# A hybrid layer on one core: the MLP seam in two column parts, norm rows further down TensorE's order, weights split ahead

## The chip, the cores and the metric

The kernel runs on one core of a Trainium2 chip. The metric is the device time of one execution in microseconds, lower is better. The times of several runs are given with their median.

## The reference

One layer of a streaming encoder in fp32, for x of 1024 tokens by 1024 channels and 256 memory tokens. There are three sub-layers, each with an RMS norm before and after it, added to the residual:

```python
# 1. token mixers on one normalised input h
q, k, v, u, gate_attn, gate_ssm = split(h @ w_in)
A = stick_breaking_attention(q, k, v)      # 8 heads x 64, strictly causal
B = s5_branch(u, ...)                      # 32 groups of 16 channels, 64 complex states each,
                                           # linear recurrence over time, GELU, y * sigmoid(y @ w_glu + b_glu)
x1 = x + norm((sigmoid(gate_attn) * (A @ w_ba) + sigmoid(gate_ssm) * (B @ w_bs)) @ w_out)
# 2. cross-attention of 4 heads x 256 into 256 memory tokens
x2 = x1 + norm(memory_cross_attention(norm(x1), mem_n, wq, wk, wv, wo))
# 3. gated MLP, d_ff = 2816, with a causal depthwise convolution of width 3 between
up = conv(norm(x2) @ w_up) + conv_b
out = x2 + norm((gelu(gate) * val) @ w_down)
```

## The kernel before

Every fp32 product is made of three TensorE passes on rounded parts (`mm3`, L139 to L142): high by high, high by low and low by high. So each weight chunk is loaded (`ws`), cast to its high part on ScalarE (ACT) (`wh`) and subtracted to its low part on VectorE (DVE) (`wl`), and each intermediate that enters a product is split the same way (`split`, L144). The names in the profile are those of the tiles: `ps_f`, `ps_z`, `ps_p` and so on are PSUM banks by tag, `hT` is the normalised input turned to channels by tokens.

Up to the end of the second sub-layer's query projection the order of TensorE, ACT, DVE and POOL is written by hand as a list of events with a planned time. `pe(took, go)` puts a TensorE step at the planner's clock and advances it; `at(t, go)` puts any other step at the time t; `plan(t, took, go, n)` puts a turn or the like into TensorE's order once the clock has come to t; `all_events` then issues all of it in order of time. The times are a plan and not a schedule: each engine runs its own instructions in the order issued, and waits where an operand isn't there.

The stages, in order: norm and turn of x with the projections to v and u; the SSM stage; the stick-breaking attention (units of a head and query blocks: scores, `weigh`); the memory's keys and values (`mem_k`, `mem_v`); the branch products with their gates; `mix_out` with w_out, in two halves of 512 tokens; the rows x1; `xa_query`; the cross attention; the output units 0 to 3 with w_o; the MLP.

In the SSM stage a slot (SLOT = 12.2 on the planner's clock) holds one of eight groups: `states` (L666, the input terms), a chain of DVE instructions with the scan (L675 to L687), `outputs` (L700, L701, which read the readout matrices F and the scanned `rc`). `operators` makes W (L602 to L604), `readout` makes F (L612 to L614), `intra` makes the part inside a chunk (L620), all on DVE first. Matmuls of the gates' projection (`gate_job`, chunks `weights`) fill TensorE between them:

```python
        def weights(self, t0, hi=5.0, lo=3.8):
            for dt_, go in ((14.0, self.load), (hi, self.high), (lo, self.low)):
                at(t0 - dt_, go)
```

The rows x1 of a half begin when its last `mix_out` step is done (`rows_x1`): x1_load, sum, square, norm rate, norm (`xr`, L1348), and then `turn_x1`, which turns the row on TensorE (L1355) and splits it (L1358, L1359). Matmuls of the next half, or of `xa_query`, stand between the turns.

In the cross attention `xa_score` and `xa_weigh` go two units apart, and `Fill` gives out filler matmuls (the query projection, or w_o of output unit 0) between their steps: `Fill(steps, 32, 16)` is two filler steps for each gap.

The MLP's up-projection is a Strassen-Winograd product of 2 x 2 blocks: seven products per pair of weight chunks (gate and value), with left operands A11, A12, S4, A22, S1, S2, S3 from the turned rows (`quad`) and right operands `bm` (L1752 for pair 0). The seam is pair 0: its products 1, 2, 5, 6, 3, 7 run in column parts, since the last output unit (unit 3) yields its tokens only now. `product(p, prod, cols)` (L1805) makes one of them: 12 matmuls (L1815, L1817, L1818) and its eviction from PSUM into `uu` (L1827 to L1834). The chain that the last part needs is: rows of unit 3 (`rows`), its two turns (`turn`, L1632) and the operands of its columns. After the seam, TensorE goes on with products of pair 1 and after it, and the convolution of pair 0 (`c_scale`, `c_tap`, `c_gelu`, L1921, L1925) runs in slots between them on ACT and DVE.

## Time and profile before

| what | value |
| --- | --- |
| three runs, median (lowest, highest) | 1708.67 us (1708.15, 1709.71) |
| profiled execution: time, span | 1710.89 us, 1709.1 us |
| mean granted TensorE clock | 0.995 of full speed |
| TensorE (PE) busy | 1658.4 us, 97% |
| VectorE (DVE) busy | 1137.8 us, 67% |
| ScalarE (ACT) busy | 865.4 us, 51% |
| GpSimd (POOL) busy | 225.3 us, 13% |

The span is from the first to the last instruction. Busy is the time in which an engine runs an instruction; TensorE's matmuls overlap, so their durations are longer than their spacing. A wait is idle time ahead of an instruction, put down to what came last. PEclk in the windows is the clock that TensorE was granted, as a share of full speed.

The stages lie at about these times: x and v, u up to 85 us; SSM from 85 to 260; attention to 568; memory to 614; branches and w_out to 802; cross attention from 831 to 976; units 1 to 3 to 1049.8; seam to 1082.3; the rest of the MLP to the end.

### The profile page before, as it was taken

The page shows a single profiled execution, that of the slowest core. Times are in us where ns is not written, and L with a number is a line of the kernel's source. Part 1 is how long each engine was busy: PE and PEld are TensorE (multiplying, and loading weights), DVE is VectorE, ACT ScalarE, POOL GpSimd, SP SyncE. Part 2 cuts the span into 40 slices and gives each one's busy share as a digit, 9 for nine tenths or more (in the row PEclk, how much of TensorE's full clock was granted, in tenths as well). Part 3 has the DMA queues.
Part 4 walks back from the last instruction along what each step waited for, and adds up shares of the span by engine and source line. Part 5 has one row for each costly group of instructions (what it writes and reads, how often), then busy time and mean ns, then how long its engine had stood idle before and what let it go on. Part 6 is the DMA issues. An engine that isn't in the chain of part 4 may idle for free.

```text
span 1709.1 us, 22655 instructions
## 1 busy us (share of the span) xinstructions
PE 1658.4 (97%) x8244; PEld 1393.4 (82%) x8244; DVE 1137.8 (67%) x1565; ACT 865.4 (51%) x1459; POOL 225.3 (13%) x247
## 2 busy tenths in 40 slices
PE   7999999999999999999999998999999999999998
PEld 6897887888888878887788887878888888788886
DVE  7718855866776655446645677788888887965473
ACT  5414444666666543235534455555555555653441
POOL 5000001433332000000221001011111111000010
PEclk9999999999999999999999999999999999999999
DMA  7002134332333774444512576386777776787572
GB/s 290 26 26 68 50 107 124 80 100 71 97 109 107 266 241 133 166 160 160 185 62 99 178 253 224 88 245 185 199 214 209 219 200 187 220 287 262 195 230 91
DMA packets 119792, 274.14 MB, mean 160 GB/s; under 512 B 21761, under 2 KB 26241, under 8 KB 119553
## 3 DMA queue, kind: packets, MB, share of 16 engines
q1 hardware_dynamic: 110320, 254.61, 44.7%
q0 software_dynamic: 9360, 18.09, 6.0%
q8 instruction: 65, 1.06, 0.3%
q14 instruction: 47, 0.38, 0.1%
HBM read 196.76 MB, written 67.37 MB: 155 GB/s over the span
## 4 chain that ended last, share of the span: by engine, by line
PE 46%; DVE 4%; DMA 2%; ACT 1%; issue 1%; POOL 0%; SPq 0%; DVEq 0%; POOLq 0%; ACTq 0%
PE ps_p L1815 7%; PE ps_p L1818 7%; PE ps_p L1817 7%; PE ps_d L2075 4%; PE ps_d L2074 4%; PE ps_d L2076 4%; PE ps_m L140 2%; PE ps_m L142 1%; PE ps_m L141 1%; PE ps_p L141 1%; PE ps_p L142 1%; PE ps_p L140 1%; PE ps_a L141 1%; PE ps_a L142 1%; PE ps_a L140 1%
## 5 line engine op out<-in xcount | busy, mean ns | idle before, releaser
L140 PE MATMUL ps_f<-hT,wh 128*128 128x512 f32 x384 | 166.8, 434 | 1.3 <-ACT wh L273 1.3
L142 PE MATMUL ps_f<-hT,wl 128*128 128x512 f32 x384 | 152.4, 397 | 3.6 <-DVE wl L277 3.6
L141 PE MATMUL ps_f<-hT,wh 128*128 128x512 f32 x384 | 151.7, 395 | 0.0
L1815 PE MATMUL ps_p<-qS,bm 128*128 128x512 f32 (+2 forms) x380 | 143.9, 379 | 3.9 <-DVE uu L1834 3.9
L1817 PE MATMUL ps_p<-qS,bm 128*128 128x512 f32 (+2 forms) x380 | 143.8, 378 | 0.0
L1818 PE MATMUL ps_p<-qS,bm 128*128 128x512 f32 (+2 forms) x380 | 143.7, 378 | 0.0
L146 DVE TENSOR_TENSOR dn<-raw,dn 128x1024 fp32r<-128x1024 f32 x77 | 93.8, 1223 | 66.5 <-ACT dn L145 64.2
L933 DVE TENSOR_TENSOR_SCAN s<-s,zcol 128x128 f32<-128x128 f32 (+3 forms) x96 | 106.4, 1109 | 37.9 <-ACT s L928 37.1
L145 ACT CAST dn<-raw 128x1024 fp32r<-128x1024 f32 x77 | 80.9, 1054 | 92.2 <-PE ps_d L2076 36.9
L939 POOL TENSOR_TENSOR s<-s,s 128x127 f32<-128x127 f32 (+4 forms) x96 | 92.2, 962 | 252.1 <-DVE s L933 208.8
L2074 PE MATMUL ps_d<-dn 128*128 128x512 f32 x308 | 119.8, 389 | 0.0
L2075 PE MATMUL ps_d<-dn 128*128 128x512 f32 x308 | 119.8, 389 | 0.0
L2076 PE MATMUL ps_d<-dn 128*128 128x512 f32 x308 | 119.8, 389 | 0.0
L1815 PE MATMUL ps_p<-qA,bm 128*128 128x512 f32 (+2 forms) x280 | 106.5, 380 | 1.7 <-DVE uu L1834 1.3
L1818 PE MATMUL ps_p<-qA,bm 128*128 128x512 f32 (+2 forms) x280 | 106.4, 380 | 0.7 <-DVE bm L1752 0.7
L1817 PE MATMUL ps_p<-qA,bm 128*128 128x512 f32 (+2 forms) x280 | 106.3, 379 | 0.0
L1764 POOL DMA_DIRECT2D bm<-in_ffn_up_T x61 | 53.4, 876 | 354.5 <-ACT bm L1763 185.6
L1829 ACT COPY uu<-ps_p 128x512 f32<-128x512 f32 (+2 forms) x93 | 52.0, 559 | 84.2 <-PE ps_p L1818 84.1
L142 PEld LDWEIGHTS ps_f<-hT,wl 128*128 128x128 f32 x384 | 72.7, 189 | 20.8 <-DVE wl L277 4.4
L1815 PEld LDWEIGHTS ps_p<-qS,bm 128*128 128x128 f32 x380 | 72.2, 190 | 17.9 <-DVE uu L1834 3.1
L209 POOL TENSOR_TENSOR rstd<-rstd,mhalf 128x1 f32<-128x1 f32 x42 | 29.2, 700 | 436.8 <-DMA raw<-td 174.0
L1818 PEld LDWEIGHTS ps_p<-qS,bm 128*128 128x128 f32 x380 | 72.1, 190 | 13.1
(520 smaller groups left out, 4469.3 us busy)
## 6 DMA issues: line engine op xcount, KB each, us to landing
raw<-sd SPq DMA_DIRECT2D x77, 256.0 KB, 3.3
bm<-in_ffn_up_T POOLq DMA_DIRECT2D x61, 256.0 KB, 5.6
ws<-in_w_in_T SPq DMA_DIRECT2D x24, 512.0 KB, 3.4
ws<-in_xa_wo_N SPq DMA_DIRECT2D x23, 512.0 KB, 4.2
wv<-in_ffn_up_T SPq DMA_DIRECT2D x22, 512.0 KB, 4.3
wg<-in_ffn_up_T SPq DMA_DIRECT2D x22, 512.0 KB, 4.1
dr<-in_ffn_down SPq DMA_DIRECT2D x22, 512.0 KB, 6.7
td<-st SPq DMA_DIRECT2D x44, 256.0 KB, 6.3
```

The costliest lines, as they stand in the source:

```text
L140: T.matmul(acc, sh, mh, start=first, stop=False)
L141: T.matmul(acc, sh, ml, start=False, stop=False)
L142: T.matmul(acc, sl, mh, start=False, stop=last)
L146: (lo or V).tensor_tensor(dl, src, f(dh), op=ALU.subtract)
L933: V.tensor_tensor_scan(s2[:, n0:n1][:, ::-1], s2[:, n0:n1][:, ::-1], zcol.to_broadcast([P, n1 - n0]), 1.0 if diag else s2[:, n1:n1 + 1], o ...
L939: G.tensor_tensor(s1[:, n0:e], s1[:, n0:e], s2[:, n0 + 1:e + 1], op=ALU.mult)
L1815: T.matmul(acc, bm[:, 0, ks], q[:, 0, k, cols], start=alone and k == 0, stop=False, skip_group_check=True)
L1817: T.matmul(acc, bm[:, 0, ks], q[:, 1, k, cols], start=False, stop=False, skip_group_check=True)
L1818: T.matmul(acc, bm[:, 1, ks], q[:, 0, k, cols], start=False, stop=k == 3, skip_group_check=True)
L2074: T.matmul(acc[i], v[:, 0, 0, sl], v[:, 0, 1], start=first, stop=False, skip_group_check=True)
L2075: T.matmul(acc[i], v[:, 0, 0, sl], v[:, 1, 1], start=False, stop=False, skip_group_check=True)
L2076: T.matmul(acc[i], v[:, 1, 0, sl], v[:, 0, 1], start=False, stop=last, skip_group_check=True)
```

## The change

- At the start, the second weight chunk's high and low part come after the first parts of `hT`.
- SSM stage: gate weights are loaded, cast and subtracted 5.2 earlier on the planner's clock. `operators(1)` and `readout(2)`, `readout(3)` come before the first slot, and each later one is a step further ahead; W has two buffers and F four. `intra` is planned at 1.75 instead of 0.5.
- The last `weigh` of the attention is held back and put behind twelve matmuls of `mem_k`. The first half of the branch weights is split 4 earlier, and the second half's loads are issued 4.1 earlier.
- x1: the chain of a row starts 5.5 instead of 8.0 ahead, its turn is planned at 8.5 instead of 6.5, the second half's pace is 5.0 instead of 4.0, and five chunks of `xa_query` instead of four run beside it.
- Cross attention: TensorE's order is by hand from its start, as it was from unit 1 of the output. The first and last group of four units give out about 1.5 filler steps per gap, so that the last group's filler also reaches the last two weighs. `rows` makes both rows of a unit in one generator, with one power on POOL.
- Seam: the column parts are (0 to 384, 384 to 512) instead of (0 to 256, 256 to 384, 384 to 512). Product 3 of the first part is made in two pieces (S4a and S4). The low operands of products 5 and 6 come after unit 3's last evictions.
- After the seam, the convolution steps of pair 0 come two slots later.

```diff
@@ -277,7 +277,7 @@
         def weights(self, t0, hi=5.0, lo=3.8):
-            for dt_, go in ((14.0, self.load), (hi, self.high), (lo, self.low)):
+            for dt_, go in ((9.0 + hi, self.load), (hi, self.high), (lo, self.low)):
@@ -439,7 +439,7 @@
             at(s0 + 2.4, lambda _, t=t: x_load(t + 4))
-    for c, (t0, t1) in enumerate(((6.3, 8.3), (7.8, 8.9), (10.4, 11.9), (12.0, 13.2))):
+    for c, (t0, t1) in enumerate(((6.3, 8.3), (9.5, 10.7), (10.4, 11.9), (12.0, 13.2))):
@@ -594,7 +594,7 @@
         pool = open_t.pool
-        wof[o] = W = pool.tile([P, 8, 8, 16], F32, tag="W", name="W")
+        wof[o] = W = pool.tile([P, 8, 8, 16], F32, tag="W", name="W", bufs=2)
@@ -607,7 +607,7 @@
         gs = slice(4 * n, 4 * n + 4)
-        fof[n] = F1 = pool.tile(sh4, F32, tag="F1", name="F1", bufs=2)
+        fof[n] = F1 = pool.tile(sh4, F32, tag="F1", name="F1", bufs=4)
@@ -749,6 +749,9 @@
     at(82.0, lambda t: readout(t, 1))
+    at(88.0, lambda t: operators(t, 1))
+    at(94.0, lambda t: readout(t, 2))
+    at(98.0, lambda t: readout(t, 3))
@@ -775,7 +778,7 @@
             if ns in first_of:
-                first_of[ns].weights(clock, *((3.8, 2.7) if ns == 64 else (5.0, 3.8)))
+                first_of[ns].weights(clock, *((3.8, 2.7) if ns == 64 else (10.2, 9.0)))
@@ -785,7 +788,7 @@
-    plan(70.0, 0.5, intra, 0)
+    plan(70.0, 1.75, intra, 0)
@@ -803,16 +806,17 @@
                 plan(s0 + SLOT, 0.9, states, n + 1)
-                if n:
-                    at(s0 + 6.4, lambda t, n=n: readout(t, n + 1))
+                if 1 <= n <= 4:
+                    at(s0 + 6.4, lambda t, n=n: readout(t, n + 3))
...
                 at(s0 + 8.5, lambda t, o=o: tables(t, o + 2))
+            if not q and o < 2:
+                at(s0 + 8.5, lambda t, o=o: operators(t, o + 2))
             if not q and o < 3:
-                at(s0 + 8.5, lambda t, o=o: operators(t, o + 1))
-                plan(s0 + SLOT, 0.5, intra, o + 1)
+                plan(s0 + SLOT, 1.75, intra, o + 1)
@@ -1042,6 +1046,7 @@
+    held = groups.pop()
@@ -1157,7 +1162,7 @@
-    at(clock + 1.2, lambda _: open_c())
+    at(clock + 3.2, lambda _: open_c())
@@ -1166,9 +1171,9 @@
         at(clock + 8.0 + 2.8 * i, lambda _, i=i: branch_load(0, i))
-        at(clock + 18.0 + 2.8 * i, lambda _, i=i: branch_high(0, i))
-        at(clock + 19.2 + 2.8 * i, lambda _, i=i: branch_low(0, i))
-        at(clock + 20.6 + 2.8 * i, lambda _, i=i: branch_load(1, i))
+        at(clock + 14.0 + 2.8 * i, lambda _, i=i: branch_high(0, i))
+        at(clock + 15.2 + 2.8 * i, lambda _, i=i: branch_low(0, i))
+        at(clock + 16.5 + 2.8 * i, lambda _, i=i: branch_load(1, i))
@@ -1215,6 +1220,8 @@
             pe(0.36, mem_k, ch, m, k)
+            if (m, k) == (0, 3):
+                pe(held[3], held[1], *held[2])
@@ -1358,12 +1365,12 @@
-    PACE = 5.4, 4.0
+    PACE = 5.4, 5.0
     def rows_x1(t, r0_):
-        line(r0_ - 8.0, (lambda: x1_load(t), 8.0), (lambda: x1_sum(t), 1.4),
+        line(r0_ - 5.5, (lambda: x1_load(t), 5.5), (lambda: x1_sum(t), 1.4),
...
-        plan(r0_ + 6.5, 0.9, turn_x1, t)
+        plan(r0_ + 8.5, 0.9, turn_x1, t)
...
@@ -1410,9 +1417,9 @@
                            for k2 in range(2) for i in range(4)]
-    for m in range(4):
+    for m in range(5):
         ch = Chunk(a["xa_wq_T"][m])
-        steady += [(ch if k == 0 else None, xa_query, (ch, m, k), False) for k in range(KT)]
+        steady += [(ch if k == 0 else None, xa_query, (ch, m // 4, m % 4, k), False) for k in range(KT)]
...
@@ -1518,27 +1528,35 @@
         ysl = yu[u][i][:, dh * 512:(dh + 1) * 512]
-        C.activation(ysl, acc[i], AF.Square, accum_out=su[u][i][:, dh:dh + 1])
+        C.activation(ysl, acc[i], AF.Square, accum_out=su[u][:, dh, i:i + 1])
...
-    def rows(u, i):
-        y, t = yu[u][i], 2 * u + i
-        xr = p6.tile([P, D], F32, tag="xn", name="xr", bufs=2)
-        dma(xr, x1_d[t])
+    def rows(u):
+        xr = [p6.tile([P, D], F32, tag="xn", name="xr", bufs=2) for _ in range(2)]
+        for i in range(2):
+            dma(xr[i], x1_d[2 * u + i])
         yield
...
+        r, o = (p6.tile([P, 2], F32, tag="r2" + n, name="r2" + n, bufs=2) for n in "ab")
+        V.tensor_tensor(r, su[u][:, 0], su[u][:, 1], op=ALU.add)
+        V.tensor_scalar(r, r, 1.0 / D, EPS, op0=ALU.mult, op1=ALU.add)
+        G.tensor_tensor(o, r, mhalf.to_broadcast([P, 2]), op=ALU.pow)
         yield
-        ss = p6.tile([P, 2], F32, tag="ss", name="ss", bufs=3)
-        C.activation(xr, y, AF.Square, accum_out=ss[:, 0:1])
...
@@ -1584,6 +1602,8 @@
+    by_hand = ctx.enter_context(ExitStack())
+    by_hand.enter_context(tc.manual_schedule(engines={mybir.EngineType.PE}))
@@ -1591,7 +1611,7 @@
-            fill = Fill(steps, 32, 16)
+            fill = Fill(steps, 32 if n else 24, 16 if n < 12 else 22)
@@ -1679,14 +1699,8 @@
     operand(hb, "hb", "A12")
-    by_hand = ctx.enter_context(ExitStack())
-    by_hand.enter_context(tc.manual_schedule(engines={mybir.EngineType.PE}))
     def both(u):
-        gs = [rows(u, 0), rows(u, 1)]
-        for _ in range(4):
-            for g in gs:
-                pump(g)
+        drain(rows(u))
@@ -1800,29 +1814,32 @@
     FULL = slice(0, 512)
+    PART = slice(0, 384), slice(384, 512)
...
-        bm, q = ops[p, prod], quad["S4a" if prod == 3 and cols.stop == 256 else LEFT[prod]]
+        bm = ops[p, prod]
+        pieces = [(quad[LEFT[prod]], cols, cols)]
+        if prod == 3 and cols == PART[0]:
+            pieces = [(quad["S4a"], slice(0, 256), slice(0, 256)), (quad["S4"], slice(256, 384), slice(256, 384))]
...
         whole = accs[p, {1: 1, 6: 1, 7: 1, 4: 1, 2: 2, 5: 5, 3: 5}[prod]]
-        acc = whole[:, cols]
         alone = prod in (1, 2, 5) or (p, prod) == (0, 4)
-        for k in range(4):
-            ks = slice(k * P, (k + 1) * P)
-            T.matmul(acc, bm[:, 0, ks], q[:, 0, k, cols], start=alone and k == 0, stop=False,
-                     skip_group_check=True)
-            T.matmul(acc, bm[:, 0, ks], q[:, 1, k, cols], start=False, stop=False, skip_group_check=True)
-            T.matmul(acc, bm[:, 1, ks], q[:, 0, k, cols], start=False, stop=k == 3, skip_group_check=True)
+        for q, to, cs in pieces:
+            for k in range(4):
+                ks, acc = slice(k * P, (k + 1) * P), whole[:, to]
+                T.matmul(acc, bm[:, 0, ks], q[:, 0, k, cs], start=alone and k == 0, stop=False, skip_group_check=True)
+                T.matmul(acc, bm[:, 0, ks], q[:, 1, k, cs], start=False, stop=False, skip_group_check=True)
+                T.matmul(acc, bm[:, 1, ks], q[:, 0, k, cs], start=False, stop=k == 3, skip_group_check=True)
...
-        src = acc.rearrange("p (c t) -> p c t", t=P)
+        src = whole[:, cols].rearrange("p (c t) -> p c t", t=P)
@@ -1849,47 +1866,44 @@
     pump(st, 4)
-    drain(pairs[0].first(5, 6))
-    g0, g1 = rows(3, 0), rows(3, 1)
-    pump(g0)
-    pump(g1)
+    l56, l37 = pairs[0].first(5, 6), pairs[0].first(3, 7)
+    pump(l56)
+    go = rows(3)
+    pump(go)
...
     unit_out(3, 1)
-    last37 = pairs[0].first(3, 7)
-    pump(last37)
-    pump(g0)
-    pump(g1)
-    PART = (slice(0, 256), slice(256, 384), slice(384, 512))
+    pump(go)
+    drain(l56)
+    pump(l37)
+    pump(go)
...
     product(0, 2, PART[0])
-    pump(g0)
-    drain(last37)
+    drain(l37)
+    pump(go)
     product(0, 5, PART[0])
-    pump(g1)
+    pump(go, 2)
     product(0, 6, PART[0])
-    drain(g0)
+    drain(go)
     product(0, 3, PART[0])
-    drain(g1)
+    drain(turn(3, 0))
     product(0, 7, PART[0])
-    drain(turn(3, 0))
-    for prod in (1, 2, 5):
-        product(0, prod, PART[1])
     st = turn(3, 1)
-    for prod in (6, 3, 7):
-        pump(st)
-        product(0, prod, PART[1])
+    pump(st, 2)
+    product(0, 1, PART[1])
+    product(0, 2, PART[1])
     pump(st)
+    product(0, 5, PART[1])
+    pump(st)
+    product(0, 6, PART[1])
+    drain(st)
+    product(0, 3, PART[1])
...
         dma(f(quad["S4"][:, j, :, 0:256]), f(quad["S4a"][:, j]))
-    product(0, 1, PART[2])
-    product(0, 2, PART[2])
-    drain(st)
-    for prod in (5, 6, 3, 7):
-        product(0, prod, PART[2])
+    product(0, 7, PART[1])
@@ -1979,29 +1993,28 @@
                 down_load(1)
-        if r == 0:
-            if done:
-                c_mul(m)
-            if live:
-                c_scale(p, 1)
-            if m > 0 and done:
-                (down_left if m % 2 else down_right)(q, 0)
-        elif r == 1 and live:
+        if r == 0 and done:
+            c_mul(m)
+        slot = r - 2 if p == 0 else r
+        if live and slot == 0:
+            c_scale(p, 1)
+        elif live and slot == 1:
             c_tap(p, 1, 1)
-        elif r == 2 and live:
+        elif live and slot == 2:
...
             c_scale(p, 0)
-        elif r == 3 and live:
+        elif live and slot == 3:
             c_tap(p, 0, 1)
...
+        elif live and slot == 4:
+            c_tap(p, 0, 2)
+        if live and slot == (4 if p == 0 else 5):
             c_gelu(p)
...
```

The first place is VectorE's order ahead of the first scan of the SSM stage, before and after in one piece (F and W are the readout and operator tiles; L675 is the scan chain's first row).

```order
+L612 TENSOR_TENSOR F_932<-pr,Y_158 128x512
+L613 TENSOR_TENSOR tq<-pi,Y_159 128x512
+L614 TENSOR_TENSOR F_932<-F_932,tq 128x512
+L612 TENSOR_TENSOR F_956<-pr,Y_158 128x512
+L613 TENSOR_TENSOR tq<-pi,Y_159 128x512
+L614 TENSOR_TENSOR F_956<-F_956,tq 128x512
+L277 TENSOR_TENSOR wl<-ws,wh 128x1024 x2
 L675 TENSOR_TENSOR bp<-ps_m,cosT 128x512
```

Two readouts and two gate weight chunks now stand ahead of the scan, and ahead of these six rows of `operators`; before, one row of L277 stood there, and the next one behind the scan.

The second place is TensorE's order in the cross attention, at the last unit's turn of its weights (`pt`) and what comes behind it. Before (`ph`, `pl` are the parts of the turned weights of one unit, `mv` the memory's values):

```order
L142 MATMUL ps_a<-ph,mv 128x256
L1574 MATMUL ps_a<-ident,pt 128x128 x4
L140 MATMUL ps_a<-ph,mv 128x256
L1574 MATMUL ps_a<-ident,pt 128x128 x4
L141 MATMUL ps_a<-pl,mv 128x256
```

The same place of the change (`wh,o` and `wl,o` are filler of output unit 0):

```order
L142 MATMUL ps_a<-ph,mv 128x256
L1592 MATMUL ps_a<-ident,pt 128x128 x4
L140 MATMUL ps_m<-wh,o_7635 128x512
L141 MATMUL ps_m<-wl,o_7635 128x512
L142 MATMUL ps_m<-wh,o_7635 128x512
```

Before, both last turns stood inside one another's weighs with no filler; now nine filler matmuls stand behind each turn.

The third place is TensorE's order in the seam, at the first turn of unit 3's rows. Before (`qS_8816` is S3, the left operand of product 7, `qA_9034` is A11, that of product 1):

```order
L1815 MATMUL ps_p<-qS_8816,bm 128x256
L1817 MATMUL ps_p<-qS_8816,bm 128x256
L1818 MATMUL ps_p<-qS_8816,bm 128x256
L1632 MATMUL ps_t<-ident,xr 128x128 x8
L1815 MATMUL ps_p<-qA_9034,bm 128x128
```

The same place of the change (`qS_9239` is S4, the second piece of product 3, `qS_8817` is S3):

```order
L1833 MATMUL ps_p<-qS_9239,bm 128x128
L1834 MATMUL ps_p<-qS_9239,bm 128x128
L1835 MATMUL ps_p<-qS_9239,bm 128x128
L1652 MATMUL ps_t<-ident,xr 128x128 x8
L1833 MATMUL ps_p<-qS_8817,bm 128x384
```

The turn stood behind product 7 of the first part; now it stands between products 3 and 7, with the 384 columns of product 7 behind it.

## Rows read from the trace of the kernel before

**Rows 1.** Page, section 1: busy us, share of the span, instructions.
```profile
PE 1658.4 (97%) x8244; PEld 1393.4 (82%) x8244; DVE 1137.8 (67%) x1565; ACT 865.4 (51%) x1459; POOL 225.3 (13%) x247
```
**Rows 2.** TensorE's waits: tile and line, for what: total us, times, longest.
```profile
PE ps_p L1815 <- DVE uu L1834: 5.2, 3, 2.7
PE ps_o L978 <- DVE wtl L965: 4.8, 4, 1.5
PE ps_f L142 <- DVE wl L277: 3.6, 2, 3.0
...
PE ps_z L140 <- ACT wh L1144: 2.3, 1, 2.3
PE ps_z L1355 <- DVE xr L1348: 1.8, 2, 1.6
PE ps_p L1815 <- ACT uu L1829: 1.8, 1, 1.8
PE ps_p L1818 <- DVE bm L1752: 1.6, 2, 0.9
PE ps_o L1355 <- DVE rstd L207: 1.5, 1, 1.5
PE ps_f L1355 <- DVE xr L1348: 1.5, 1, 1.5
PE ps_f L140 <- ACT wh L273: 1.3, 1, 1.3
PE ps_f L140 <- ACT hT L407: 1.2, 1, 1.2
PE ps_a L1574 <- DVE o L146: 1.1, 1, 1.1
PE ps_m L620 <- DVE W L604: 1.0, 2, 0.8
...
PE ps_w L1355 <- DVE xr L1348: 0.9, 1, 0.9
PE ps_a L140 <- ACT ph L145: 0.7, 1, 0.7
PE ps_z L142 <- DVE wl L1147: 0.7, 1, 0.7
```
**Rows 3.** Windows: length; busy PE, PEld, DVE, ACT, POOL; PEclk; DMA share; GB/s.
```profile
128.20:170.90 42.70, 38.89 (x225) 33.86 (x226) 36.77 (x62) 17.44 (x22) 0.43 (x4) 0.93 0.21 68
139.70:196.24 56.54, 53.76 (x316) 46.20 (x315) 54.38 (x96) 28.98 (x35) 0.84 (x5) 0.97 0.21 67
580.00:620.00 40.00, 37.02 (x210) 31.86 (x210) 23.13 (x20) 23.00 (x28) 3.68 (x4) 1.00 1.00 322
1049.80:1140.00 90.20, 82.59 (x461) 71.79 (x460) 70.83 (x103) 49.44 (x92) 10.09 (x13) 0.96 0.54 160
```
**Rows 4.** Timeline of ACT in the memory stage: start, duration, instruction, idle before.
```profile
614.20 1.04 ACT L1107 CAST oh<-stb 128x1024 fp32r<-128x1024 f32 x1 [5.56 <-DMA stb<-ol_d]
```
**Rows 5.** Timeline of TensorE: matmuls of 384, 256 and 128 columns.
```profile
281.20 0.34 PE L917 MATMUL ps_z<-k,q 128*128 128x384 f32 x1
281.37 0.33 PE L918 MATMUL ps_z<-kl,q 128*128 128x384 f32 x1
...
1052.55 0.28 PE L1815 MATMUL ps_p<-qA,bm 128*128 128x256 f32 x1
...
1053.98 0.28 PE L1815 MATMUL ps_p<-qS,bm 128*128 128x256 f32 x1
...
1064.92 0.27 PE L1817 MATMUL ps_p<-qA,bm 128*128 128x128 f32 x1
...
1065.93 0.28 PE L1817 MATMUL ps_p<-qA,bm 128*128 128x128 f32 x1
```
**Rows 6.** Timeline of DVE behind the seam.
```profile
1094.24 1.28 DVE L1925 SCALAR_TENSOR_TENSOR cg<-uu,cw,cg 128x1023 f32<-128x1023 f32 x1 [0.71 <-ACT cg L1921]
1095.45 0.68 DVE L1834 TENSOR_TENSOR uu<-ps_p,uu 128x512 f32<-128x512 f32 x1
```

More of the change, by code (lines that the diff above doesn't have):

```diff
@@ L1388, with xa_query @@
     q2, o2 = {}, [None] * 4
-    def xa_query(now, ch, m, k):
+    def xa_query(now, ch, hp, m, k):
         if k == 0:
@@ L1399, in high @@
             if m == 0:
-                q2[0, 0] = ha.tile([P, 2, 4, 512], F32R, tag="ha", name="q2_00")
-            C.copy(q2[0, 0][:, 0, m], acc)
+                q2[0, hp] = ha.tile([P, 2, 4, 512], F32R, tag="ha", name=f"q2_0{hp}")
+            C.copy(q2[0, hp][:, 0, m], acc)
         at(now + 0.9, high)
-        at(now + 1.6, lambda _: V.tensor_tensor(q2[0, 0][:, 1, m], acc, f(q2[0, 0][:, 0, m]), op=ALU.subtract))
+        at(now + 1.6, lambda _: V.tensor_tensor(q2[0, hp][:, 1, m], acc, f(q2[0, hp][:, 0, m]), op=ALU.subtract))
     steady = []
@@ L1438 @@
         pe(took, turn_, x)
-    first_q = [Chunk(a["xa_wq_T"][4 + m]) for m in range(2)]
+    first_q = [Chunk(a["xa_wq_T"][5 + m]) for m in range(2)]
     for m, ch in enumerate(first_q):
@@ L1452, in xa_q @@
     def xa_q(h, hp):
-        q2[h, hp] = qt = ha.tile([P, 2, 4, 512], F32R, tag="ha", name=f"q2_{h}{hp}")
-        for m in range(4):
+        m0 = (h, hp) == (0, 1)
+        if not m0:
+            q2[h, hp] = ha.tile([P, 2, 4, 512], F32R, tag="ha", name=f"q2_{h}{hp}")
+        qt = q2[h, hp]
+        for m in range(m0, 4):
             ch = first_q.pop(0) if first_q else None
@@ L1492, in unit @@
         yu[u] = [p6.tile([P, D], F32, tag="y", name="y", bufs=4) for _ in range(2)]
-        su[u] = [p6.tile([P, 2], F32, tag="ss2", name="ss2", bufs=8) for _ in range(2)]
+        su[u] = p6.tile([P, 2, 2], F32, tag="ss2", name="ss2", bufs=4)
         seq = [(dh, c) for dh, *chunks in plan for c in chunks]
@@ L1520, in unit_out @@
         ysl = yu[u][i][:, dh * 512:(dh + 1) * 512]
-        C.activation(ysl, acc[i], AF.Square, accum_out=su[u][i][:, dh:dh + 1])
+        C.activation(ysl, acc[i], AF.Square, accum_out=su[u][:, dh, i:i + 1])
         V.tensor_tensor(ysl, acc[i], gap[:, dh * 512:(dh + 1) * 512], op=ALU.mult)
     xn_of = {}
-    def rows(u, i):
-        y, t = yu[u][i], 2 * u + i
-        xr = p6.tile([P, D], F32, tag="xn", name="xr", bufs=2)
-        dma(xr, x1_d[t])
+    def rows(u):
+        xr = [p6.tile([P, D], F32, tag="xn", name="xr", bufs=2) for _ in range(2)]
+        for i in range(2):
+            dma(xr[i], x1_d[2 * u + i])
         yield
-        r = rstd_of(p6, su[u][i], two=True)
-        V.scalar_tensor_tensor(y, y, r, xr, op0=ALU.mult, op1=ALU.add)
-        dma(x2_d[t], y)
+        r, o = (p6.tile([P, 2], F32, tag="r2" + n, name="r2" + n, bufs=2) for n in "ab")
+        V.tensor_tensor(r, su[u][:, 0], su[u][:, 1], op=ALU.add)
+        V.tensor_scalar(r, r, 1.0 / D, EPS, op0=ALU.mult, op1=ALU.add)
+        G.tensor_tensor(o, r, mhalf.to_broadcast([P, 2]), op=ALU.pow)
         yield
-        ss = p6.tile([P, 2], F32, tag="ss", name="ss", bufs=3)
-        C.activation(xr, y, AF.Square, accum_out=ss[:, 0:1])
+        for i in range(2):
+            V.scalar_tensor_tensor(yu[u][i], yu[u][i], o[:, i:i + 1], xr[i], op0=ALU.mult, op1=ALU.add)
+            dma(x2_d[2 * u + i], yu[u][i])
         yield
-        r = rstd_of(p6, ss)
-        V.scalar_tensor_tensor(xr, y, r, gfp, op0=ALU.mult, op1=ALU.mult)
-        xn_of[u, i] = xr
+        ss = [p6.tile([P, 2], F32, tag="ss", name="ss", bufs=4) for _ in range(2)]
+        for i in range(2):
+            C.activation(xr[i], yu[u][i], AF.Square, accum_out=ss[i][:, 0:1])
+            yield
+        for i in range(2):
+            r = rstd_of(p6, ss[i])
+            V.scalar_tensor_tensor(xr[i], yu[u][i], r, gfp, op0=ALU.mult, op1=ALU.mult)
+            xn_of[u, i] = xr[i]
+            yield
     s3 = [P, 2, 256]
```

14 lines of the change are left out of this document (6 added, 8 removed).

## Prediction

> **What bounds the kernel now.** I read the page's busy times first: TensorE is busy 97% of the span, no other engine over 67% [rows 1]. So time can only come from matmul time itself, from TensorE's idle time, and from stretches at the lower of its two clock levels (1.2 and 2.4 GHz). The table of waits gives the idle time: no wait is large, and the sixteen of [rows 2] add up to 31 us. They stand at few places: the SSM stage (waits for `wl` and `wh` of L277 and L273, and `W` of L604), the last weigh of the attention and the memory stage (`wtl`, and `wh` and `wl` of L1144 and L1147), the x1 rows (`xr`, `rstd`), the end of the cross attention (`o`, `ph`) and the MLP seam with what follows it (`uu`, `bm`). The windows add the clock: 0.93 over 42.7 us of the SSM stage, which is 3.0 us of full speed lost, and 0.96 over the 90.2 us from the seam on, 3.6 us [rows 3]. Both stretches hold two drops, of some 1.7 us each, and each begins right behind a wait. The wait of 2.3 us for `wh` L1144 in the memory stage has no drop behind it (1.00 from 580 to 620), so I don't count a drop for every wait.
>
> **The change, part by part.**
>
> *Head.* The low and high parts of the second weight chunk move behind the first `hT` parts. That aims at the 1.2 us wait for `hT` L407 [rows 2]. The ACT casts in front of it are gone, DVE's and the next chunk's remain: I take 0.8, with bounds 0 and 1.2.
>
> *SSM stage.* The gate weights are split 5.2 us earlier, with the load moved by the same 5.2, so load and cast keep their distance, and on SP's queue the loads pass a few of the gates' stores; operators and two readouts go into the quiet stretch before the first scan. That aims at 3.6 + 1.3 + 1.0 = 5.9 us of waits and 3.0 of clock, 8.9 together. But DVE is busy 54.38 of 56.54 us over four slots [rows 3], 13.6 a slot, and the change takes none of this work out of the slots: it shifts each slot's readout by two, and the last operators drop out only at the end. TensorE's slot is (56.54 - 2.8 of waits - 1.7 of clock) / 4 = 13.0, and with `intra` at 1.75 instead of 0.5 the planner puts six 512-column matmuls less into three of four slots, at 0.17 x 512 / 384 = 0.23 each [rows 5], 1.0 a slot on the mean: 12.0. DVE is then behind by 1.6 a slot, and what is late next is `rc`, which the output matmuls read. It shows in three slots, 1.6 in two and 1.2 in the last, which is relieved of its operators: 4.4 us of new waits. Gain 8.9 - 4.4 = 4.5; bounds 1 (DVE sets every slot and one drop stays) and 8.9 (the work done ahead covers all). The matmuls moved out aren't saved: they stand before the GLU.
>
> *Held weigh, branch weights.* The last weigh goes behind twelve matmuls of the memory's keys: these cover the `wtl` wait, at most 1.5 [rows 2], I take 1.4. `wh` of L1144 (2.3) and `wl` (0.7) wait because the ACT queue stands at L1107 for a transfer, 5.56 us idle [rows 4]; the cast of the branch weights is queued behind it. Four microseconds earlier it stands ahead of it. Of the 3.0 I take 2.6. Against: the DMA share from 580 to 620 is 1.00 [rows 3], so a load that is wanted sooner may land no sooner, and the second half's branch loads are issued four microseconds sooner into the same share; bounds for both together 1 and 4.5.
>
> *x1 rows.* Loads start later against the rows, but the turns stand further down and one more chunk of the query projection stands before the last of them. First half: 1.8 + 0.9 for `xr` [rows 2]. The turns move by nine matmuls, 2.1 us, but the pace goes with them and DVE's norm still stands behind the split of the memory's keys: I take 0.4. Second half: 1.5 + 1.5, where the extra chunk, five instead of four, puts more matmuls ahead of the last turn; its own split is queued on the same DVE, so of the 3.0 I take 1.7. Together 2.1; bounds 0 and 5.7.
>
> *Cross attention.* The last group of units keeps filler for the last two weighs, where TensorE now waits 1.1 for `o` and 0.7 for `ph` [rows 2]: 1.8. The price: nine matmuls of filler in a gap instead of twelve, in the first four and the last four units; 0.6 us less cover in each, and I count 1.1 in all. Gain 0.7; bounds -3 and 1.8. Two `rstd` of a row pair become one, on POOL, which is busy 13% [rows 1].
>
> *Seam.* Three column parts become two. Rows: a 256-column matmul every 0.119 us (1.43 over 12), a 128-column one every 0.112 (1.01 over 9), a 384-column one every 0.17 [rows 5]. Before: 72 x 0.119 + 144 x 0.112 = 24.7. After: 60 x 0.17 + 12 x 0.119 + 84 x 0.112 = 21.0. Saved 3.7.
>
> The Trainium skill (TensorE: Matmul & The Clock Gate, Back-to-back issue gap) gives 81 ns for a weight load with 128 columns, and 162 ns for 384 columns by its formula for one matmul alone. By these it would be 19.5 before and 17.9 after, a saving of 1.6 instead of 3.7. The rows are of these same fp32 passes, so they decide.
>
> The seam's waits are 1.8 for `uu` L1829 and 1.6 for `bm` [rows 2]. They stand at product 3's first part, which came after 48 matmuls at 0.119 and now comes after 48 at 0.17: 2.4 us more cover. I leave 1.1 of new waits for the piece of `S4` that is now read there: 2.3 gained, and one drop of 1.7. Behind the seam TensorE waits for `uu` L1834, longest 2.7 [rows 2]: DVE ran a convolution step of 1.28 just ahead of that eviction [rows 6]. These steps come two slots later for pair 0, so the eviction is early by that 1.28 and the idle time before it; I leave 1.1 and count 1.6, and the second drop, 1.7. Seam: 3.7 + 2.3 + 1.7 + 1.6 + 1.7 = 11.0; bounds 3.7 and 13.
>
> **Sum.** 0.8 + 4.5 + 4.0 + 2.1 + 0.7 + 11.0 = 23.1. The profiled execution took 1710.89, 2.2 above the median of the three runs; 1710.9 - 23.1 = 1687.8, and against the median 1685.6.
>
> **The rivals.**
>
> 1. *DVE never binds and all the waits go.* 1.2 + 8.9 + 4.5 + 5.7 + 1.8 + 13 = 35: 1674. For it: the two readouts and the operators done ahead are a stock that four slots may not use up. Against: 54.38 of 56.54 us is 96% [rows 3], and the work per slot stays.
>
> 2. *The seam gives only its matmuls.* With parts of 384 columns the first evictions and the row chain of unit 3 come in larger lumps, product 3 still waits, both drops stay: 23.1 - 2.3 - 1.7 - 3.3 = 15.8, 1693. For it: the chain of unit 3 (norm, S1, S2, S3, S4) has to be done 3.7 us sooner.
> The Trainium skill (Perfetto Trace Analysis, Optimizing Scalar/DVE Operations) says that where ScalarE and VectorE are not saturated but hold up others, breaking work up lets it finish sooner; this change joins parts. DVE is busy 70.83 and ACT 49.44 of the 90.2 us [rows 3], so the rule's condition holds; what it would make of the time is this rival.
>
> 3. *The stages before don't pay.* DVE binds every SSM slot with a drop left, and the branch weights, at a DMA share of 1.00, land when they did: 4.5 - 1 and 4.0 - 1.4 go, and the x1 rows give 0: 23.1 - 8.2 = 14.9, 1694.
>
> 4. *Slower: the order by hand in the cross attention.* If TensorE's fixed order meets the softmax chain at each weigh as it now does at the last ones, a unit costs 1.1 + 0.7 = 1.8, sixteen units 28.8, of which 1.8 are there already: 23.1 - 0.7 - 27 = -4.6, 1713. It decides from (22.4 + 1.8) / 16 = 1.5 us a unit. For it: an order by hand can't fill a gap with other work. Against: units 4 to 11 have the same rows in the same order as before, and of sixteen units only the last ones' waits for `o` and `ph` are among the larger ones [rows 2].
>
> **How the numbers follow.** Forecast 0.55; rival 1 0.13; rival 2 0.15; rival 3 0.13; rival 4 0.04. The likeliest gives 1686, with its own range 1680 to 1692 from the bounds of the SSM slots and the seam. The range to hold the time 8 times in 10 takes in rivals 2 and 3 and ends at rival 1: 1674 to 1697. What a measurement can tell from no change is about 0.2%, 3.4 us. All cases but the fourth are faster by more; some of it lies where several parts fail together: faster 0.93, same 0.03, slower 0.04.
>
> **What would show it.** Right: the waits for `wl` L277, `W` and `wh` L273 are gone and new ones for `rc` stand at the SSM's outputs, 1 to 2 us each; PEclk near 1.00 in both windows; `wh` L1144 no longer in the table of waits; 384-column matmuls every 0.17 us in the seam, which is some 8 us shorter; one wait of about 1 us for `uu` behind it. Wrong: new waits at the weighs of the cross attention; a clock below 1.00 in a new place; the wait for `wh` L1144 merely turned into one for its transfer. The prediction fails most easily on the SSM slots, whose new waits are only worked out, and on the seam's chain, which the trace shows in another order.

## The result, and the profile after

The changed kernel takes 1689.8 us (median of 4 runs, 1688.31 to 1691.54), the kernel before 1709.19 (1708.15 to 1711.18): a ratio of 0.9886, interval 0.9868 to 0.9903, so 1.1% faster. The forecast was 1686. The profiled executions stand further apart than the medians, 1710.89 and 1688.58: 22.3 us, where the sum of the prediction was 23.1 against this same execution of before; by the medians it is 19.4. The sum came out; its terms did so only in part, and that they add up so well is luck: two stretches gave 1.7 and 1.6 us more than forecast, the other four together 4.0 less. By the starts of TensorE's matmuls in the two traces (the GLU is the gated product that ends the SSM branch):

| stretch, ended by | before | after | gained | forecast |
| --- | --- | --- | --- | --- |
| head and SSM: first matmul of the GLU | 238.93 | 231.94 | 7.0 | 5.3 |
| attention to branches: first `mix_out` | 706.94 | 696.08 | 3.9 | 4.0 |
| x1 rows: first score of the cross attention | 831.38 | 822.31 | 3.7 | 2.1 |
| cross attention, units 1 to 3: first seam product | 1049.82 | 1037.10 | -1.8 | 0.7 |
| seam: first 512-column product of pair 1 | 1082.31 | 1062.70 | 6.9 | 7.7 |
| behind the seam, to the end | 1702.18 | 1679.88 | 2.7 | 3.3 |

In the third and fourth rows I have moved 5.5 us, the 24 matmuls of the fifth query chunk at 0.23 each, to where they stood before. By rounding, the rows add up to 22.4.

TensorE's busy time on the page of the changed kernel (as [rows 1]):

```profile
PE 1649.6 (98%) x8184; PEld 1386.4 (82%) x8184; DVE 1132.4 (67%) x1558; ACT 862.6 (51%) x1453; POOL 222.4 (13%) x242
```

Its waits in the changed kernel (as [rows 2]; L982 was L978, L1152 was L1147, L1833 to L1835 were the three matmuls of a product, L1846 to L1851 its evictions):

```profile
PE ps_m L404 <- DVE xn L398: 8.4, 2, 7.9
PE ps_p L141 <- DMA wl<-wol: 3.7, 3, 1.5
PE ps_o L982 <- DVE wtl L969: 3.5, 4, 1.4
PE ps_o L141 <- DVE wl L1152: 2.1, 2, 1.7
PE ps_f L140 <- ACT glog L302: 1.9, 1, 1.9
PE ps_p L1834 <- DVE qS L1660: 1.7, 2, 1.5
PE ps_f L142 <- DVE rstd L207: 1.4, 1, 1.4
...
PE ps_p L1833 <- ACT uu L1846: 1.2, 2, 0.7
PE ps_p L1833 <- DVE uu L1851: 1.1, 1, 1.1
...
PE ps_m L701 <- DVE rc L687: 1.0, 1, 1.0
PE ps_f L1362 <- DVE y L1325: 0.9, 1, 0.9
PE ps_p L140 <- DVE y L1532: 0.8, 1, 0.8
```

The waits for `wl` L277, `W`, `wh` L273 and `wh` L1144 are gone, those for `xr`, `o` and `ph` too. New are `glog`, `rc`, `qS` and `y` L1532, a second wait for `xn` L398 at the start (0.5), a wait for `wl` L1152 at `mix_out` (1.7 of the 2.1), and a third wait for the stored parts of w_o. The windows (as [rows 3]) show the clock back in the SSM stage and VectorE still almost always busy there. A drop, below, is a stretch in which the granted clock was at the lower of its two levels, 1.2 instead of 2.4 GHz:

```profile
128.20:170.90 42.70, 40.41 (x258) 35.32 (x257) 40.53 (x71) 19.61 (x25) 0.42 (x4) 1.00 0.19 63
135.00:195.00 60.00, 56.75 (x346) 49.16 (x346) 56.23 (x101) 30.52 (x38) 0.53 (x5) 1.00 0.19 63
570.00:610.00 40.00, 39.55 (x228) 34.30 (x227) 23.91 (x21) 23.52 (x29) 3.67 (x4) 1.00 0.99 323
1037.10:1127.30 90.20, 87.26 (x444) 75.10 (x443) 76.04 (x108) 54.30 (x95) 10.91 (x13) 0.98 0.61 178
```

In the memory stage ScalarE's timeline (as [rows 4]) shows the cast of the branch weights (602.25) now ahead of the one that waits for a transfer. That wait is still there, 4.38 us, at a DMA share of 0.99; nobody on TensorE waits behind it:

```profile
602.25 1.05 ACT L1149 CAST wh<-ws 128x1024 fp32r<-128x1024 f32 x1
607.67 1.05 ACT L1112 CAST oh<-stb 128x1024 fp32r<-128x1024 f32 x1 [4.38 <-DMA stb<-ol_d]
```

In the seam a 384-column matmul comes every 0.175 us (4.20 over 24 in TensorE's timeline, as [rows 5]):

```profile
1041.46 0.33 PE L1833 MATMUL ps_p<-qS,bm 128*128 128x384 f32 x1
...
1045.66 0.28 PE L1833 MATMUL ps_p<-qS4a,bm 128*128 128x256 f32 x1
```

### The profile page after: what moved, and what is told of

It reads as the page before. It is cut to its first block, busy times and chain, and to the rows that moved or that the text cites. A ratio compares the mean times of both kernels' runs of the same rounds, so it can differ in the third digit from the quotient of the medians.

```text
span 1686.8 us, 22509 instructions
## 1 busy us (share of the span) xinstructions
PE 1649.6 (98%) x8184; PEld 1386.4 (82%) x8184; DVE 1132.4 (67%) x1558; ACT 862.6 (51%) x1453; POOL 222.4 (13%) x242
## 4 chain that ended last, share of the span: by engine, by line
PE 46%; DVE 4%; DMA 2%; ACT 2%; issue 1%; POOL 0%; DVEq 0%; POOLq 0%; ACTq 0%
PE ps_p L1833 7%; PE ps_p L1835 7%; PE ps_p L1834 7%; PE ps_d L2088 4%; PE ps_d L2087 4%; PE ps_d L2089 4%; DMA wl<-wol 1%; PE ps_m L140 1%; PE ps_m L141 1%; PE ps_m L142 1%; PE ps_p L141 1%; PE ps_a L141 1%; PE ps_p L142 1%; PE ps_p L140 1%; PE ps_a L142 1%
## 5 line engine op out<-in xcount | busy, mean ns | idle before, releaser
L1834 PE MATMUL ps_p<-qS,bm 128*128 128x512 f32 (+2 forms) x368 | 140.5, 382 | 1.7 <-DVE qS L1660 1.7
L1833 PE MATMUL ps_p<-qS,bm 128*128 128x512 f32 (+2 forms) x368 | 140.7, 382 | 1.3 <-ACT uu L1846 1.2
L1835 PE MATMUL ps_p<-qS,bm 128*128 128x512 f32 (+2 forms) x368 | 140.4, 382 | 0.0
L937 DVE TENSOR_TENSOR_SCAN s<-s,zcol 128x128 f32<-128x128 f32 (+3 forms) x96 | 102.5, 1068 | 42.0 <-ACT s L932 41.1
L943 POOL TENSOR_TENSOR s<-s,s 128x127 f32<-128x127 f32 (+4 forms) x96 | 95.8, 1001 | 253.5 <-DVE s L937 210.0
L1833 PE MATMUL ps_p<-qA,bm 128*128 128x512 f32 (+2 forms) x272 | 105.3, 387 | 1.1 <-DVE uu L1851 1.1
L1835 PE MATMUL ps_p<-qA,bm 128*128 128x512 f32 (+2 forms) x272 | 105.1, 386 | 0.0
L1834 PE MATMUL ps_p<-qA,bm 128*128 128x512 f32 (+2 forms) x272 | 105.0, 386 | 0.0
L1846 ACT COPY uu<-ps_p 128x512 f32<-128x512 f32 (+2 forms) x90 | 51.4, 571 | 82.4 <-PE ps_p L1835 82.4
L1833 PEld LDWEIGHTS ps_p<-qS,bm 128*128 128x128 f32 x368 | 69.2, 188 | 15.5 <-ACT uu L1846 2.0
L1834 PEld LDWEIGHTS ps_p<-qS,bm 128*128 128x128 f32 x368 | 69.3, 188 | 15.1 <-DVE qS L1660 2.0
L140 PEld LDWEIGHTS ps_f<-hT,wh 128*128 128x128 f32 x384 | 73.4, 191 | 8.4 <-ACT glog L302 2.4
```

Source lines behind the costliest of these rows:

```text
L140: T.matmul(acc, sh, mh, start=first, stop=False)
L937: V.tensor_tensor_scan(s2[:, n0:n1][:, ::-1], s2[:, n0:n1][:, ::-1], zcol.to_broadcast([P, n1 - n0]), 1.0 if diag else s2[:, n1:n1 + 1], o ...
L943: G.tensor_tensor(s1[:, n0:e], s1[:, n0:e], s2[:, n0 + 1:e + 1], op=ALU.mult)
L1833: T.matmul(acc, bm[:, 0, ks], q[:, 0, k, cs], start=alone and k == 0, stop=False, skip_group_check=True)
L1834: T.matmul(acc, bm[:, 0, ks], q[:, 1, k, cs], start=False, stop=False, skip_group_check=True)
L1835: T.matmul(acc, bm[:, 1, ks], q[:, 0, k, cs], start=False, stop=k == 3, skip_group_check=True)
```

## The experiments

Each kernel is the changed one with the edit shown. Times are medians, ratios are against the kernel before on the same chip; the changed kernel's is 0.9886. Since the runs of one kernel lie 2 to 7 us apart from lowest to highest, I read each edit's size from the traces, by the starts of the same matmuls, and the ratio says whether the whole agrees.

**Three parts of the SSM edit.**

```diff
 e1: -  ... else (10.2, 9.0)))            +  ... else (5.0, 3.8)))
 e2: operators(1), readout(2), readout(3) no longer ahead, later ones a step later
 e3: -  plan(..., 1.75, intra, ...)       +  plan(..., 0.5, intra, ...)
```

> The changed kernel with the gate weights of the SSM stage split as late as before (cast 5.0 and subtraction 3.8 ahead of their chunk). Theory: the early split is what took away the waits for wl (L277) and wh (L273), 4.8 us of them before, and the two clock drops of 1.7 us each that followed; some of it overlaps with the 3.3 us that the changed kernel now waits in these slots. So 3 to 7 us slower than the changed kernel, some 1692 to 1696, with those waits back in the table and PEclk under 1.00 in the SSM stage. Rival: it was the operators and readouts done ahead that freed VectorE's queue, and the weights would come in time anyway: 0 to 1 us slower.

> The changed kernel with operators and readouts where they were, none ahead of the first slot and each one step later. Theory (VectorE's work per slot is the same, only the deadline moves): the waits for W (L604), 1.0 us before, come back at intra, perhaps with one clock drop of 1.7: 1 to 3 us slower than the changed kernel. Rival (the early split of the gate weights did it all): no difference, within 0.5 us.

> The changed kernel with intra planned at 0.5 as before, so that six more matmuls stand in three of the slots and fewer ahead of the GLU. Theory (VectorE sets the slots, and TensorE's 3.3 us of waits there are lack of work): these matmuls fill the waits, 1.5 to 3 us faster than the changed kernel, the waits in the stage under 1.5 us. Rival (the later intra is what keeps the waits for W away): the waits for W come back, 1 us and perhaps a clock drop of 1.7, so 0 to 2 us slower.

Measured: e1 1696.28 (0.9925, 0.9912 to 0.9939), its GLU 9.6 us later than the changed kernel's; e2 1694.57 (0.9913, 0.9900 to 0.9926), 6.0 later; e3 1689.12 (0.9881, 0.9867 to 0.9896), 0.04 earlier. By the medians e1 is 6.5 and e2 4.8 us slower than the changed kernel. TensorE's waits, first the row that came back in e1:

```profile
PE ps_f L142 <- DVE wl L277: 7.5, 3, 3.6
```

A window of e1 over the SSM slots shows the drops behind these waits, 0.09 x 60 = 5.4 us of full speed:

```profile
125.00:185.00 60.00, 53.42 (x302) 45.78 (x302) 52.34 (x93) 25.26 (x32) 0.53 (x5) 0.91 0.18 57
```

The row that came back in e2:

```profile
PE ps_m L620 <- DVE W L604: 2.4, 2, 1.6
```

The row of e3 that stands in place of the changed kernel's three waits in the slots:

```profile
PE ps_m L701 <- DVE rc L687: 2.1, 1, 2.1
```

Both early edits are needed, and at the GLU each alone undone costs more than expected. Drops make up more than half of both: about 5 of the 9.6, and 3.3 of the 6.0 in e2 (0.11 x 30 us, from 180 to 210). The rest is waits: 8.1 us in the slots of e1, where the kernel before, with neither edit, has 5.8. I take it that with VectorE's queue filled by the one edit, the other's rows come later than they did before; no run tests that by itself. e3 falls between: the intra matmuls did fill the small waits, and no wait for `W` came back, but one larger wait for `rc` stands in their place with a clock drop behind it, and the stage ends at the same time. A bound by VectorE would look like that; e12 below tests it.

**What holds ScalarE's eviction.**

```diff
-    logs.append((pa, "vt", 1))
+    logs.append((pa, "vt", 2))
```

> The changed kernel with two buffers instead of one for the gate's result (tag vt), whose store held up ScalarE's eviction L302 and so the 1.95 us wait of TensorE for a bank. Theory (VectorE sets the slots): the wait goes from there and comes back at the next two outputs as a wait for rc; the time stays within 0.5 us. Rival (the wait for the buffer adds to the rest): 1.9 us faster and the wait for rc stays at 1.0.

Measured: 1688.12 (0.9878, 0.9865 to 0.9892); the GLU starts 0.12 us sooner. The time is as the theory said, but not for its reason. TensorE's waits in e4 still have the row:

```profile
PE ps_f L140 <- ACT glog L302: 1.9, 1, 1.9
```

So the buffer isn't what holds L302. ScalarE's timeline in the changed kernel shows what does: the waves of the next tables and two copies for the turned outputs are queued ahead of it. They came late because ScalarE itself stood idle for 3.70 us until VectorE had made `x` (L585), so this wait, too, goes back to VectorE's queue; in e3 and e12 it is gone.

```profile
148.43 1.06 ACT L588 ACTIVATE cosT<-x 128x1024 f32<-128x1024 f32 x1 [3.70 <-DVE x L585]
...
150.80 1.06 ACT L589 ACTIVATE sinT<-x 128x1024 f32<-128x1024 f32 x1
151.76 1.14 ACT L590 ACTIVATE cosT<-cosT,hpi 128x1024 f32<-128x1024 f32 x1
152.81 2.01 ACT L719 COPY U<-ps_m 128x512 f32<-128x512 f32 x2
154.61 0.67 ACT L302 ACTIVATE glog<-ps_f,bgate 128x512 f32<-128x512 f32 x1
```

**Seam.**

```diff
 e5, in turn:      -  low("S3", u, t3)             e6: PART = (0, 256), (256, 384), (384, 512),
                   -  low("S4", u, s4)                 products of parts two and three
                   +  low("S4", u, s4)                 in the old order
                   +  low("S3", u, t3)             e9: slot = r for pair 0 too
```

> The changed kernel with S4's low operand subtracted ahead of S3's in a turn. Product 3 of the last part waits 1.52 us for S4's low half, which VectorE makes as the second of two (1.29 us), behind S3's, and after an idle 0.60 for S3's high half. Theory: S4's low half is ready 1.2 us sooner, the wait falls to 0.4 or less, product 7, twelve matmuls of 0.112 later, finds S3 ready, and the clock drop that begins with this wait is gone as well: 1.2 us faster, or 2.9 with the drop. Rival: the wait moves to product 7: no gain.

> The changed kernel with the seam in three column parts (256, 128, 128) again, in the old order of the products, everything else as changed (the row pair's chain, the low halves of products 5 and 6 after the evictions, the convolution two slots later). Theory: 3.7 us of matmul time come back (72 at 0.119 and 144 at 0.112 against 60 at 0.17, 12 at 0.119 and 84 at 0.112), and the waits for product 3's first part (1.8 and 0.9 before), less the 1.7 that the changed kernel waits for S4: 4 to 6 us slower than the changed kernel. Rival: the spacing that the Trainium skill gives for a weight load with 128 columns (81 ns): 1.6 us slower by the matmuls alone.

> The changed kernel with the convolution steps of pair 0 in their old slots. Theory of the prediction: these steps two slots later are what lets the eviction L1851 through, so the 2.7 us wait behind the seam comes back, with its drop 1.6 to 3.3 us slower. Rival: with three column parts that wait stood there in spite of the later slots, so the two column parts took it away, and the slots do nothing: within 0.5 us, and no wait over 1 us behind the seam that the changed kernel doesn't have.

Measured: e5 1688.10 (0.9884, 0.9871 to 0.9898); e6 1695.49 (0.9929, 0.9916 to 0.9942); e9 1688.78 (0.9879, 0.9864 to 0.9895). In e5 the wait for `qS` fell from 1.52 to 0.40 and the drop didn't come; the seam was 1.5 us shorter. But 1.5 for the eviction L1848 came in its place at pair 1, more at evictions further on, and all of it was lost by the start of the down-projection. TensorE's waits in e5:

```profile
PE ps_p L1833 <- ACT uu L1848: 1.5, 1, 1.5
...
PE ps_p L1834 <- DVE qS L1660: 0.6, 2, 0.4
```

In e6 the seam alone took 29.4 us against 25.6, with nearly the same waits (1.9 and 1.7), so 3.8 for two parts in place of three, the 3.7 of matmul time. By the spacing in the Trainium skill (TensorE: Matmul & The Clock Gate, Back-to-back issue gap) the estimate was 1.6; the trace doesn't agree. Another 4.4 us were lost behind the seam: TensorE's timeline in e6 has the wait for `uu` back, and a clock drop begins with it.

```profile
1079.15 0.79 PE L1833 MATMUL ps_p<-qS,bm 128*128 128x512 f32 x1 [2.72 <-DVE uu L1851]
```

It is back although the convolution steps were at their later slots. And in e9, with these at their old slots, it is not there: no wait over 0.3 us in its place, and 407.1 us from pair 1 to the down-projection, 407.6 in the changed kernel. The one larger wait for `uu` in e9's table (1.1) stands at the end of the up-projection, where the kernel before and the changed one have 1.3 and 1.1.

```profile
PE ps_p L1833 <- DVE uu L1851: 1.3, 2, 1.1
```

So it is the two column parts that took this wait away. VectorE's own order is set by the scheduler there; in e9 it is the same row for row, but for buffer numbers, as in the changed kernel, and in e6 the convolution stands ahead of L1851 as in [rows 6].

**Cross attention, branches, x1 rows.**

```diff
 e7:  no order by hand before unit 1;  Fill(steps, 32 if n else 24, 16)
 e8:  branch_high(0) at 18.0, branch_low(0) at 19.2, branch_load(1) at 20.6
 e10: line(r0_ - 8.0, ...), plan(r0_ + 6.5, ...), PACE = 5.4, 4.0
```

> The changed kernel with TensorE's order in the cross attention left to the scheduler and 32 filler steps over 16 gaps in each group but the first (24), as before; the fifth query chunk stays where the change put it. Theory: in the changed kernel the cross attention and the units up to the seam lose 1.8 us against before, by fewer matmuls in a gap and by the waits for the stored w_o parts, though the last weighs gain 1.9; with this undone the waits for ph and o come back (1.9) and the small ones for pl (0.7) go: within 1 us of the changed kernel. Rival: the order by hand is what costs, 2 us or more faster without it.

> The changed kernel with the first half's branch weights split 4 later and the second half's loads 4.1 later, as before; the held weigh stays. Theory: ScalarE's cast stands behind the one that waits for the attention's low part from memory again, and TensorE's waits for wh and wl come back: 2.3 + 0.7 = 3.0, less the 0.45 that is there now: 2 to 3 us slower. Rival: what took the wait away is the held weigh and the transfer that came sooner with the shorter stages before: 0 to 0.5.

> The changed kernel with the x1 rows as before: chain 8.0 ahead, turn planned at 6.5, pace 4.0 in the second half; the fifth query chunk stays. Theory: TensorE's turns stand further up again and wait for xr and rstd, 3.5 us in the first half and up to 3.0 in the second, in place of the 1.7 for wl, 0.9 for y and 1.4 for rstd that the changed kernel has there: 2 to 3 us slower. Rival: VectorE is the limit in the first half's rows, so the waits only change places, and the extra query chunk covers the second half: 0 to 1 us.

Measured: e7 1688.70 (0.9890, 0.9875 to 0.9906), from the first score to the seam 213.8 us, 1.0 shorter than in the changed kernel; e8 1693.79 (0.9915, 0.9901 to 0.9928), its `mix_out` 2.9 later; e10 1693.86 (0.9914, 0.9901 to 0.9927), 3.6 longer over the x1 rows. TensorE's waits in e8 (of the first row 0.95 stands at the branches, the other 1.75 at `mix_out`, as in the changed kernel):

```profile
PE ps_o L141 <- DVE wl L1152: 2.7, 2, 1.8
PE ps_o L140 <- ACT wh L1149: 2.2, 1, 2.2
```

TensorE's waits in e10, at the turns of the x1 rows:

```profile
PE ps_z L1362 <- DVE xr L1355: 1.8, 2, 1.6
...
PE ps_o L1362 <- DVE rstd L207: 1.5, 1, 1.5
PE ps_f L1362 <- DVE xr L1355: 1.5, 1, 1.5
...
PE ps_w L1362 <- DVE xr L1355: 0.9, 1, 0.9
```

These are the waits of before, in both. In e7 the waits for `ph` and `o` came back, 0.7 and 1.5, with a drop, and still the stretch was shorter: the waits for `y` and `pl` went, and two of three for the stored w_o.

```profile
PE ps_p L141 <- DMA wl<-wol: 1.9, 1, 1.9
...
PE ps_a L1592 <- DVE o L146: 1.5, 1, 1.5
...
PE ps_a L140 <- ACT ph L145: 0.7, 1, 0.7
```

But 1.0 us is no finding here. The ten other runs that keep this part of the change and have no drop in the stretch took 213.5 to 215.8 us over it, with 2.4 to 4.0 us of waits for the stored w_o; the changed kernel's 214.8 and e7's 213.8, with its drop of 1.7, both lie within. e7 also keeps the smaller filler of the first group and the new `rows`, so it tests only the order by hand and the last group's filler.

**Less for VectorE.**

```diff
 e11: the gates' wl from the second on: V -> G;   t0 = clock + 31.0 + 5.5 * ... (keys and values);   e5's edit
 e12: e3's edit, and
+    at(102.0, lambda t: operators(t, 2))
+    at(107.0, lambda t: readout(t, 4))
 ... three buffers for W, five for F; the later operators and readouts one step further ahead
```

> The changed kernel with work taken from VectorE or moved in three stages that the trace tells apart. SSM: the low parts of all gate chunks but the first on GpSimd (2.4 us each there, 1.2 on VectorE). x1 rows: the split of the memory's keys and values 11 later. Seam: S4's low operand ahead of S3's. Theory (VectorE sets the SSM slots and the rows of the first half): with 1.2 us less on VectorE in each slot, TensorE's 3.3 us of waits in the SSM stage fall to 1 or less, 2 to 3 us sooner at the GLU; the waits of 1.7 for wl and 0.9 for y in the first half's rows fall to 1 or less in all, 1.6 or more; the seam gains what its run alone showed, next to nothing. Together 4 to 5 us faster than the changed kernel, 1685. Rival for the SSM stage: the wait behind ScalarE's gate eviction L302 (1.95) is its own and stays, as it did with two buffers: 1 us there. Rival for the rows: the keys' split is not in the way: 0.

> The changed kernel with intra planned at 0.5 as before, and with operators(2) and readout(4) put into the quiet stretch before the first slot as well (three buffers for W, five for F), so that VectorE has 3.9 us less to do between the scans of the third and the fourth slot. With intra at 0.5 alone the stage waited once, 2.07 us for rc, with a clock drop behind it, and came out at the same time as the changed kernel. Theory (VectorE's work in the slots sets the stage): that wait and its drop go, and the GLU comes 2.5 to 3.7 us sooner than in the changed kernel: some 1686 to 1687. Rival (ScalarE's evictions, or TensorE's own order of states, hold the stage): a wait as long stands elsewhere in the slots, and the GLU comes within 0.5 us of before.

Measured: e11 1691.16 (0.9896, 0.9881 to 0.9911), where 1685 was expected, its GLU 2.4 us later, not sooner, the x1 rows 0.7 longer (the first half gained 0.9 of waits, the second lost 0.6). e12 1685.67 (0.9861, 0.9844 to 0.9878), its GLU 4.0 us sooner. The timeline of e11 shows the reason on VectorE: while GpSimd subtracts for 2.40 us, a pair of instructions takes 3.60 that takes 1.38 elsewhere.

```profile
139.01 3.60 DVE L688 TENSOR_TENSOR bt<-r,sinT 64x508 f32<-64x508 f32 x2
139.68 2.40 POOL L277 TENSOR_TENSOR wl<-ws,wh 128x1024 fp32r<-128x1024 f32 x1 [20.41 <-ACT wh L273]
```

At GpSimd's next subtract an L605 took 2.84 instead of 0.68, and at the one behind it an L616 took 2.74 instead of 0.69:

```profile
186.25 2.74 DVE L616 TENSOR_TENSOR F<-F,tq 128x512 f32<-128x512 f32 x1
```

So VectorE lost 2.1 to 2.2 us three times to save 1.2 each, and its busy time from 135 to 195 rose from 56.2 to 58.3 us. The same window of e12 as for the changed kernel above:

```profile
135.00:195.00 60.00, 60.00 (x363) 52.47 (x363) 52.35 (x94) 30.69 (x38) 0.83 (x5) 1.00 0.21 68
```

TensorE is busy for all 60 us and VectorE for 52 instead of 56. More time on VectorE took the stage 2.4 later, less work 4.0 sooner (expected 2.5 to 3.7), and in e12 none of the waits in the slots is left: VectorE's work in the slots did set it. e12 beats both kernels in median and in its lowest and highest run (1684.69 to 1686.87); its interval overlaps the changed kernel's.

## Why the prediction was right, and where it wasn't

*Head, 0.8 forecast, 0.4 found.* The wait of 1.2 for `hT` L407 went, but 0.5 for `xn` L398 came a little further on.

*SSM, 4.5 forecast, 6.6 found (7.0 less 0.4 of the head).* The old waits and both drops went, as forecast. The drops were worth 3.4 rather than 3.0, since the window of [rows 3] ends inside the second one (from 128.2 to 176.0 the clock is 0.93 as well). The step that VectorE then falls behind by 1.6 a slot was right in kind (e11, e12) and mis-sized: 3.3 us of new waits instead of 4.4. Only 1.0 of them is for `rc`; I hadn't seen that ScalarE's queue would hold a bank for 1.9. That leaves 5.9 + 3.4 - 3.3 = 6.0; three waits in place of five give most of the rest, since a wait costs more than its row shows (see the x1 rows).

*Memory stage, 4.0 forecast, 3.9 found.* The cast passed the waiting one, and e8 gives 2.9 of it back when it doesn't. The held weigh has no run of its own; the `wtl` waits fell by 1.3 in the trace, 1.4 forecast. Rival 3's doubt, a DMA share of 1.00, didn't matter, since the cast no longer stood behind that transfer.

*x1 rows, 2.1 forecast, 3.7 found.* Mis-sized: the first half gained 0.9 rather than 0.4 (waits of 1.7 for `wl` and 0.9 for `y` in place of 3.5), the second 1.7 in waits, as forecast. The other 1.1 is what a wait costs beyond its row. Here, in the changed kernel, starts that are otherwise 0.23 apart come 2.08 and 0.33 apart, which is 1.95 late for a row of 1.69:

```profile
764.09 0.39 PE L140 MATMUL ps_o<-wh,mh 128*128 128x512 f32 x1
766.17 0.50 PE L141 MATMUL ps_o<-wl,mh 128*128 128x512 f32 x1 [1.69 <-DVE wl L1152]
766.50 0.40 PE L142 MATMUL ps_o<-wh,ml 128*128 128x512 f32 x1
```

Seven waits became three in this stretch, and four times 0.26 is 1.0. e10 has the whole of it, 3.6.

*Cross attention, 0.7 forecast, -1.8 found.* The last weighs' 1.8 was gained. Against it stand 0.8 for `y` L1532 and 0.4 more for `pl`, 1.3 more for the stored w_o, and some 1.1 that is in no wait. Of this, two waits more at 0.26 are 0.5, and spacings too short for a row, such as 0.49 at 983.81, are most of the rest. The step that failed is the price: I counted only less cover by filler (1.1) and no new wait. Rival 4, at 28.8, was far too large; whether the order by hand costs anything stays open, since e7 can't tell, and the -1.8 is itself no surer than the 2 us by which this stretch differs between runs.

*Seam, 7.7 forecast, 6.9 found.* The matmul term held, 3.7 against 3.8 in e6. Of new waits I left 1.1, it was 1.7, all for `S4` and `S1` low halves, and not where I looked: the piece of `S4` in the first part came in time, product 3 of the last part waited. The clock drop, which I took as gone, begins 2.3 us behind that wait and falls on pair 1. Of the old 1.6 for `bm`, 0.7 stood at product 2 and not at product 3; it went all the same.

*Behind the seam, 3.3 forecast, 2.7 found, and the step itself was wrong.* I gave it to the convolution steps two slots later. They do nothing (e9); the two parts did it, as e6 shows. Rival 2, that the seam gives only its matmuls, is refuted for the changed kernel.

## What to carry to other kernels

Where a second engine is 96% busy over a stretch, taking away the first one's waits there soon uncovers it: count its work per step, and move work to quiet time ahead of the stretch, as e12 does. Undoing one of two edits that share a queue can leave more waits than undoing both (8.1 us in e1, 5.8 before). A wait costs more than its row, here some 0.26 us, and shorter ones have no row: compare starts of the same matmuls. And before a gain is put to moved source lines, look at whether the engine's order moved with them.
